# Weight halves kept in DRAM instead of split again: a hybrid S5 / delta-net / ConvFFN step on one core

## The chip, the core and the metric

The kernel runs on one core of a Trainium2 chip. The engines are named as in the profile: PE multiplies matrices (PEld is its weight load), DVE, ACT and POOL work element by element, SP only issues DMAs; 16 DMA engines move data between DRAM and the on-chip memory. The metric is the device time of one launch in microseconds (us). Before the change three runs took 2869.67, 2872.86 and 2876.55 us; their median is 2872.86.

## The reference

One layer of a decoder step on 2048 prompt tokens and 8 sample tokens, all in float32:

```
n = rmsnorm(x);  proj = n @ w_in                       # 1024 -> 2568 columns
y_s5  = s5_mixer(proj[:, :512])                        # state space scan, then gelu and a gate (s5_w_glu)
y_gdn = gdn_mixer(proj[:, 512:])                       # q, k, v, z of 4 heads: delta rule in chunks
x = x + concat(y_s5, y_gdn) @ w_out                    # 1024 x 1024
h = causal_conv(rmsnorm(x) @ w_up)                     # 1024 -> 2 * 2816, width 3
y = rmsnorm(x + (silu(h_gate) * h_up) @ w_down)        # 2816 -> 1024
```

The states of the scan, of the delta rule and of the convolutions are outputs too.

## The kernel before

The prompt is worked in four quarters of 512 tokens; quarter 0 carries the 8 samples behind its tokens and is multiplied in two blocks of 256 and 264 columns, the others in one of 512. Norm 1 and the S5 inputs of all quarters come first, then the S5 batches beside the delta net of quarter 0, then (from about 560 us) the output gate, output projection and FFN of one quarter after the other, with the delta net of the next quarters beside them. The orders of emission are the strings `PRE`, `MIXERS` and `FFN`; a scheduler that simulates the engines makes the order of each queue from them, so the order on an engine is fixed before the kernel runs.

A float32 product is made of three matmuls on two halves of each operand: hi (rounded) and lo (the rest), hi*hi + hi*lo + lo*hi (`mm3`, L287 to L289). Weights come in tiles of 128 x 1024. For each use of a tile `wsplit` loads the raw tile into `wr` (512 KB, issued by SP from L303 for columns of a matrix, from L1082 for rows of w_down), ACT copies it to `whi` (L71), and DVE, or POOL in the early part, subtracts to get `wlo` (L72). There are 2 buffers `wr` and 8 buffers for halves, so 4 tiles split and 2 raw ones ahead. A tile is used for 24 matmuls of 512 columns (48 half as wide in quarter 0). Each quarter loads and splits its tiles anew:

- w_in for q, k, v and z of 4 heads: 16 tiles per quarter (`gdn_front`);
- the gate s5_w_glu: 4 tiles for each two quarters (`s5_glu`);
- w_out: 8 tiles for each half of a quarter's tokens (`ffn_out`), so 16 per quarter;
- w_up: 44 tiles and w_down: 22 tiles per quarter (`ffn`, `ffn_down`). In quarters 1 to 3 four of the w_up tiles are used for the first half of the tokens and once more for the second (`UPS`).

With the 4 tiles of the S5 input that makes 404 splits. The buffers for halves (`c.W`) also hold other things: `gdn_sample` (L984) puts the samples' states (`S0s`, 4 loads for a first product and 4 more for the new states) and `vd` into them, `sample_halos` its raw rows. SP's queue works in order: an issue whose buffer isn't free holds all behind it, the small DMAs of the delta net's inverse (`nD`, `N`, `xD`, `T2T`, `gdn_inverse`) among them.

Of the kernel before, what the change touches and what calls it, by code (L numbers as in the profile page):

```python
# [20 lines left out]
QT = 512            # tokens per quarter  # L21
NQ = QT + 8         # the first quarter carries the 8 samples behind its tokens
NCH = 256           # S5 chunks of 8 tokens
# [14 lines left out]
# order of emission. u: next tile of the S5 input projection, l: samples' halos, c: columns of the first  # L38
# quarter; b, h: first and second part of the next S5 batch, x: S5 samples; F, I, B: front, inverse and back
# of the next delta net head, N: norm and columns of the next quarter, S: delta net samples, G: final states;  # L40
# r: next piece of the output gate, the output projection and the FFN
# [3 lines left out]
# columns of the constants  # L45
# [3 lines left out]
def f32(ap):  # L49
    return ap.bitcast(F32)  # L50
# [18 lines left out]
def split(nc, hi, lo, raw, eng=None):  # L69
    """hi + lo == raw exactly, both float32r."""  # L70
    nc.scalar.activation(hi, raw, AF.Copy)  # L71
    (eng or nc.vector).tensor_tensor(lo, raw, f32(hi), op=OP.subtract)  # L72


def sigmoid_(nc, out, x, scale=1.0):
    """out = sigmoid(scale*x) by exp and ln; 1/(1+inf) = 0 comes out of exp(-ln inf)."""
    nc.scalar.activation(out, x, AF.Exp, scale=-scale)
    nc.scalar.activation(out, out, AF.Ln, bias=1.0)
    nc.scalar.activation(out, out, AF.Exp, scale=-1.0)


def rsqrt_(nc, a, y, t):
    """y = a^-1/2; one Newton step after exp/ln."""
# [9 lines left out]
def rsqrt_cols(c, ss, n, scale, tag, rows=128, tmp=None):  # L93
    """(ss*scale + eps)^-1/2 for ss [rows, n]"""
# [6 lines left out]
# ---------------------------------------------------------------- constants  # L101
def consts(c):
# [13 lines left out]
    # per-channel weights as columns  # L116
# [17 lines left out]
    # GDN  # L134
# [4 lines left out]
    # w_in columns for beta, a: [hi 8 | lo 8] per k tile  # L139
# [15 lines left out]
    # Xi[p, r, i] = (i == 4 (p % 8) + r): four rows of a 32 x 32 identity per partition  # L155
# [8 lines left out]
def sample_halos(c):  # L164
    """contribution of the samples' conv states to their conv outputs: [channel, sample]"""
# [24 lines left out]
# ---------------------------------------------------------------- norm 1  # L190
def norm_split(c, nT, kt, src, g, rsB, b0, b1):
    """nT[kt] <- hi, lo of src * g[channel] * rsB[token]"""
# [13 lines left out]
def norm_first(c, q, nT, xs):  # L206
    """x^T and its row scales to DRAM, x^T times the channels' weights into nT; the row scales are
    in it only in the first quarter, elsewhere they come after the projection"""
# [26 lines left out]
    # row scales on all partitions  # L235
# [13 lines left out]
def norm_samples(c, pre):  # L249
    """normed x^T of the samples, [channel, (k tile, sample)]"""  # L250
# [41 lines left out]
def wsplit(c, src, eng=None):  # L292
    """[128, 1024] of weights as hi and lo"""
    hi, lo, wr = c.W("whi"), c.W("wlo"), c.WR("wr")
    src(wr)
    split(c.nc, hi, lo, wr, eng or c.wl)
    return hi, lo


def wcols(c, w, col, q=None):  # L300
    """w[:, col:col+128] as hi and lo, [128, k, 128]"""
    def load(wr):
        (q or c.nc.sync).dma_start(wr.rearrange("p (k f) -> p k f", k=8), w.rearrange("(k p) f -> p k f", p=128)[:, :, col:col + 128])  # L303
    return [t.rearrange("p (k f) -> p k f", k=8) for t in wsplit(c, load)]
# [7 lines left out]
def proj(c, q, nT, w, col):  # L312
    """w[:, col:col+128]^T n, one PSUM tile per block of tokens"""
# [12 lines left out]
# ---------------------------------------------------------------- S5  # L326
def cmul(nc, pool, outr, outi, ar, ai, br, bi, shape, tag):
    """(outr + i outi) = a*b; outputs must not alias inputs."""
# [16 lines left out]
def s5_setup(c):  # L345
    """S5 matrices to DRAM: per batch of 4 groups T, F (input), E (output), tables."""
# [5 lines left out]
    c.ab1 = cp.tile([128, 2, 32], F32, name="ab1")   # re | signed im (-, +)  # L352
    with tc.tile_pool(name="s5b", bufs=1, side="right") as sp:
# [3 lines left out]
        def dup_T(ap, name):  # L357
            """[32, 64] dram -> [128 (n twice), 32]"""
# [18 lines left out]
        # angle to [-pi, pi]  # L377
# [18 lines left out]
        # powers of a-bar: PR, PI [128, 32, 9]  # L396
# [13 lines left out]
        # f  # L410
# [14 lines left out]
        # W = f B  [128 (n twice), 32, 16]  # L425
# [9 lines left out]
        # C transposed [128 (n twice), 512 (g c)]  # L435
# [13 lines left out]
        # signed power tables  # L449
        PA = sp.tile([128, 32, 9], F32, name="PA")  # L450
        PB = sp.tile([128, 32, 9], F32, name="PB")
        QA = sp.tile([128, 32, 8], F32, name="QA")   # powers 7 .. 0
# [14 lines left out]
        # d on the diagonal: rows 112..127 of K_0  # L467
# [7 lines left out]
        for b in range(8):  # L475
# [4 lines left out]
            def outer(eng, dst, x, xp, y, yp):  # L480
                # dst[p, g, l, c] = x[p, g, c]*xp[p, g, l] + y[p, g, c]*yp[p, g, l]
# [7 lines left out]
            FTs = st("FTs")   # [.., g, s, c'] = a^(7-s) f B  # L489
# [14 lines left out]
            pT = ps("s")    # [(s c'), j, g, c]  # L504
# [6 lines left out]
        # rotation tables  # L511
# [9 lines left out]
        for b in range(4):  # L521
            gs = slice(8 * b, 8 * b + 8)
            CSt = sp.tile([128, 2, 8, 65], F32, name="CSt")     # cos | signed sin (+ | -)
# [14 lines left out]
def s5_in(c, q, nT, pre, ws, rsB):  # L538
    """u to DRAM, time as (position in chunk, chunk)"""
# [19 lines left out]
def s5_states(c, sp):  # L559
    """samples: inputs and states of all groups"""  # L560
# [6 lines left out]
    c.h0 = sp.tile([128, 2, 32, 8], F32, name="h0")      # [re | im , im | re]  # L567
# [13 lines left out]
def s5_gelu(c, sp, out, y, rows=128):  # L581
    """gelu(y) = y sigmoid(2 sqrt(2/pi) (y + 0.044715 y^3))"""
# [13 lines left out]
def s5_turn(c, e, Ct, St, out):  # L596
    """out = the states e of a quarter's end, rotated back"""
# [10 lines left out]
def s5_batch(c, t, sp):  # L608
    """4 groups (64 channels) over all prompt tokens, and their samples"""
# [19 lines left out]
    # chunk inputs, rotated  # L629
# [13 lines left out]
    # scans in place, a quarter at a time  # L643
# [8 lines left out]
    # the rotation back of the last state, and of the states in two parts for the two products with E  # L652
# [5 lines left out]
    # outputs  # L658
# [13 lines left out]
    # samples  # L672
# [13 lines left out]
def s5_sample(c, sp):  # L686
# [5 lines left out]
    # new state = x + a h0  # L692
# [20 lines left out]
def s5_glu(c, q0, yT):  # L713
    """output gate of two quarters"""
# [12 lines left out]
    for a in range(4):  # L727
# [5 lines left out]
        h4, l4 = (v(t) for t in wsplit(c, load))  # L733
# [25 lines left out]
# ---------------------------------------------------------------- gated delta net  # L759
def gdn_cols(c, q, nT):  # L760
    """per-token columns: 0 beta, 1 g, 2 -gc, 3 e^gc, 4 e^(gl-gc), 5 e^gl, 6 -e^gc"""
# [26 lines left out]
    nc.vector.scalar_tensor_tensor(t_, m_, -2.0, xa_, op0=OP.mult, op1=OP.add)   # -|x|  # L788
# [20 lines left out]
def gdn_front(c, q, h, nT, col, hp):  # L809
    """projections, conv, norms, decay: L^T, A^T, scaled k and v of one head"""  # L810
# [31 lines left out]
    # transposes to token-major  # L842
# [11 lines left out]
    # head columns: 0 rk, 1 rq*d^-1/2, 2 nk, 3 -rk^2 beta, 4 rk e^(gl-gc), 5 beta rk, 6 rq'^2/128  # L854
# [14 lines left out]
    # decay  # L869
# [20 lines left out]
def gdn_inverse(c, h, LT, T):  # L890
    """(I - L)^-1 transposed for the 4 chunks of a head: 32-blocks by substitution (four rows of a
    block per partition), then merged to 64 and 128."""
# [18 lines left out]
    # merge 32 -> 64 -> 128  # L911
# [33 lines left out]
def gdn_back(c, q, h, col, F, T):  # L945
    """chunk recurrence, output norm and gate of one head"""
# [20 lines left out]
    # output norm and gate  # L967
# [16 lines left out]
def gdn_sample(c, col):  # L984
    """one step of the delta rule for the 8 samples of all heads; columns are (head, sample)"""
# [6 lines left out]
    # kS, qS  # L992
# [10 lines left out]
    # sums over channels, and per-sample scalars, on every partition  # L1003
# [11 lines left out]
    # v_new = beta (v - e^g rk kS)  # L1015
# [4 lines left out]
    # o = rq' (e^g qS + (q.k) rk v_new)  # L1020
# [5 lines left out]
    # norm and gate  # L1026
# [7 lines left out]
    # states: e^g S + k v_new^T  # L1034
# [30 lines left out]
def sample_conv_out(c, new, nt, old, out):  # L1065
    """conv states of the samples: the old one shifted, and the new row"""
# [13 lines left out]
# ---------------------------------------------------------------- output projection and FFN  # L1080
# [373 lines left out]
```

## Time and profile before

| | |
|---|---|
| median of three runs | 2872.86 us |
| span of the profiled execution | 2874.3 us |
| PE busy | 2715.0 us, 94% |
| DVE busy | 2176.9 us, 76% |
| ACT busy | 1476.0 us, 51% |
| DMA, mean of the span | 115 GB/s |

The profiled execution's span is 1.4 us above the median of the runs and inside their range. PE is busy for nearly the whole of the stretches inside a quarter from about 840 us on; its granted clock there is 1.00 of its full speed. Before that, in the S5 and first delta net part, both are lower. The boundaries between the quarters of the FFN lie near 1300 to 1440, 1900 to 2000 and 2400 to 2480 us.

### The profile page before, as it was taken

Reading aid. Unit: us, or ns where it says so; the run is one execution under the profiler, and the core shown is the slowest. Engines: PE = TensorE matmul, PEld = TensorE weight load, DVE = VectorE, ACT = ScalarE, POOL = GpSimd, SP = SyncE. Lnnn points to the kernel's source line nnn. Section 1 sums busy time; section 2 is a strip of 40 time slices with the busy share of each in tenths; the row PEclk is TensorE's granted clock in tenths of the full one; section 3 lists DMA queues with packets and bytes.
Section 4 is the critical chain, followed back from the end, with each engine's and each line's share of the span. In section 5 each row is a group of like instructions: output and inputs, shape, how many; then the busy total and the mean of one; then the engine's idle time right before and its main releaser. Section 6 shows DMA issues by size and latency. Waiting matters only on the chain.

```text
span 2874.3 us, 45554 instructions
## 1 busy us (share of the span) xinstructions
PE 2715.0 (94%) x16103; PEld 2337.9 (81%) x16103; DVE 2176.9 (76%) x4964; ACT 1476.0 (51%) x3051; POOL 609.6 (21%) x970
## 2 busy tenths in 40 slices
PE   6998788899999999998899999999999998999998
PEld 4798676786888999998887888878888787888887
DVE  8949898856688787778588687887768667676666
ACT  4446565653665554455564554555545445444444
POOL 4325332100121122222221100113211112211112
PEclk9999887898999999999999999999999999999999
DMA  7644433453644232233533333245333334523332
GB/s 205 199 134 132 113 109 92 105 133 104 182 110 117 77 103 87 89 97 111 155 115 109 100 91 98 84 137 174 93 96 97 90 93 144 157 88 96 95 97 74
DMA packets 457657, 329.30 MB, mean 115 GB/s; under 512 B 74960, under 2 KB 412249, under 8 KB 457412
## 3 DMA queue, kind: packets, MB, share of 16 engines
q1 hardware_dynamic: 447091, 297.77, 35.8%
q0 software_dynamic: 10336, 28.61, 3.4%
q8 instruction: 127, 2.08, 0.3%
q14 instruction: 103, 0.84, 0.1%
HBM read 279.29 MB, written 47.29 MB: 114 GB/s over the span
## 4 chain that ended last, share of the span: by engine, by line
PE 66%; DVE 17%; DMA 8%; ACT 4%; issue 3%; POOL 0%; SPq 0%; DVEq 0%; POOLq 0%; ACTq 0%
PE psmm L287 15%; PE psmm L288 15%; PE psmm L289 15%; PE psd L287 5%; PE psd L288 5%; PE psd L289 5%; DVE wlo L72 3%; DVE t L823 1%; ACT whi L71 1%; DVE X L907 1%; DMA xr<-xTD 1%; DMA mr<-mixT 1%; DVE x L1097 1%; DVE hh L649 1%; DMA wr<-in_w_out_dram 1%
## 5 line engine op out<-in xcount | busy, mean ns | idle before, releaser
L287 PE MATMUL psmm<-nT,whi 128*128 128x512 f32 (+2 forms) x3232 | 1115.5, 347 | 45.2 <-ACT whi L71 9.6
L288 PE MATMUL psmm<-nT,whi 128*128 128x512 f32 (+2 forms) x3232 | 1110.3, 344 | 4.8 <-DVE nT L224 3.0
L289 PE MATMUL psmm<-nT,wlo 128*128 128x512 f32 (+2 forms) x3232 | 1107.2, 343 | 1.7 <-POOL wlo L72 1.0
L287 PEld LDWEIGHTS psmm<-nT,whi 128*128 128x128 f32 x3232 | 622.5, 193 | 120.3 <-ACT whi L71 11.7
L288 PEld LDWEIGHTS psmm<-nT,whi 128*128 128x128 f32 x3232 | 624.5, 193 | 73.1 <-DVE nT L224 4.5
L71 ACT ACTIVATE whi<-wr 128x1024 fp32r<-128x1024 f32 x404 | 427.2, 1059 | 496.3 <-PE psmm L288 309.9
L289 PEld LDWEIGHTS psmm<-nT,wlo 128*128 128x128 f32 x3232 | 623.0, 193 | 72.4 <-issue 1.9
L72 DVE TENSOR_TENSOR wlo<-wr,whi 128x1024 fp32r<-128x1024 f32 x388 | 482.3, 1246 | 193.2 <-ACT whi L71 187.4
L1097 DVE TENSOR_TENSOR x<-psd,x 128x512 f32<-128x512 f32 (+2 forms) x464 | 255.6, 558 | 127.3 <-PE psd L289 125.2
L287 PE MATMUL psd<-gt,whi 128*128 128x512 f32 (+2 forms) x928 | 323.6, 350 | 12.7 <-DVE x L1097 10.4
L288 PE MATMUL psd<-gt,whi 128*128 128x512 f32 (+2 forms) x928 | 316.5, 342 | 0.0
L289 PE MATMUL psd<-gt,wlo 128*128 128x512 f32 (+2 forms) x928 | 314.6, 340 | 0.0
L1254 DVE SCALAR_TENSOR_TENSOR t<-raw,cc,t 128x512 f32<-128x512 f32 x352 | 271.5, 772 | 37.1 <-ACT t L1251 27.5
L1255 POOL COPY halo<-raw 128x2 f32<-128x2 f32 x176 | 49.6, 282 | 850.7 <-DVE raw L1250 765.9
L1251 ACT ACTIVATE t<-raw,cc 128x512 f32<-128x512 f32 (+1 forms) x176 | 127.2, 723 | 170.0 <-DVE raw L1250 156.7
L287 PEld LDWEIGHTS psd<-gt,whi 128*128 128x128 f32 x928 | 175.0, 189 | 42.5 <-DVE x L1097 18.8
L72 POOL TENSOR_TENSOR gt<-s,gt 128x512 fp32r<-128x512 f32 (+1 forms) x88 | 134.7, 1531 | 350.4 <-ACT gt L71 341.6
L288 PEld LDWEIGHTS psd<-gt,whi 128*128 128x128 f32 x928 | 175.1, 189 | 20.6
L289 PEld LDWEIGHTS psd<-gt,wlo 128*128 128x128 f32 x928 | 174.9, 189 | 20.8
L1107 POOL TENSOR_TENSOR sq<-sq 128x256 f32<-128x256 f32 (+1 forms) x112 | 109.8, 981 | 219.1 <-ACT sq L1105 213.1
L906 DVE TENSOR_TENSOR tm<-X,N 128x124 f32<-128x124 f32 (+30 forms) x496 | 125.4, 253 | 26.7 <-DMA N<-nD 17.6
L907 DVE TENSOR_TENSOR X<-X,tm 128x124 f32<-128x124 f32 (+30 forms) x496 | 129.6, 261 | 8.4
(503 smaller groups left out, 3666.5 us busy)
## 6 DMA issues: line engine op xcount, KB each, us to landing
wr<-in_ffn_w_up_dram SPq DMA_DIRECT2D x176, 512.0 KB
wr<-in_ffn_w_down_dram SPq DMA_DIRECT2D x88, 512.0 KB
wr<-in_w_in_dram SPq DMA_DIRECT2D x64, 512.0 KB
wr<-in_w_out_dram SPq DMA_DIRECT2D x64, 512.0 KB
xTD<-xT SPq DMA_DIRECT2D x32, 256.0 KB
N<-nD SPq DMA_DIRECT2D x16, 512.0 KB
mr<-mixT SPq DMA_DIRECT2D x32, 256.0 KB
xr<-xTD SPq DMA_DIRECT2D x32, 256.0 KB
```

The lines of the kernel that those rows point to most:

```text
L71: nc.scalar.activation(hi, raw, AF.Copy)
L72: (eng or nc.vector).tensor_tensor(lo, raw, f32(hi), op=OP.subtract)
L287: nc.tensor.matmul(out, lhsT=wh, rhs=xh, start=first, stop=False)
L288: nc.tensor.matmul(out, lhsT=wh, rhs=xl, start=False, stop=False)
L289: nc.tensor.matmul(out, lhsT=wl, rhs=xh, start=False, stop=last)
L906: nc.vector.tensor_tensor(m, X[:, :, j:j + 1].to_broadcast(sh), N[:, j:j + 1, j + 1:].to_broadcast(sh), op=OP.mult)
L907: nc.vector.tensor_tensor(X[:, :, j + 1:], X[:, :, j + 1:], m, op=OP.add)
L1097: nc.vector.tensor_tensor(x2[:, j, b0:b1], p, x2[:, j, b0:b1], op=OP.add)
L1107: c.nc.gpsimd.tensor_tensor(acc[0], acc[0], s, op=OP.add)
L1251: nc.scalar.activation(t[:, :n], raw[:, 2:2 + n], AF.Copy, scale=w[2])
L1254: nc.vector.scalar_tensor_tensor(t[:, :QT], raw[:, j:j + QT], w[j], t[:, :QT], op0=OP.mult, op1=OP.add)
L1255: nc.gpsimd.tensor_copy(c.halo[:, ch], raw[:, QT:QT + 2])
```

## The change

A hi and a lo half now share one buffer of 128 x 2 x 1024, of which there are 4 (`c.W2`). The first time that a tile of w_in (q, k, v, z), s5_w_glu, w_up or w_down is split, SP also stores both halves to a DRAM tile of 1 MB; when a later quarter asks for the same tile, one DMA of 1 MB loads both halves, and there is no raw load and no split. That makes 86 stores and 250 loads of halves. w_out and the S5 input's tiles are not kept: they are loaded raw and split as before. What used one of the 8 buffers (`S0s`, `vd`, the raw rows of `sample_halos`) now takes the first half of one of the 4. Comments are dropped too, so line numbers shift by 8 or so.

```diff
-def wsplit(c, src, eng=None):
-    hi, lo, wr = c.W("whi"), c.W("wlo"), c.WR("wr")
-    src(wr)
-    split(c.nc, hi, lo, wr, eng or c.wl)
-    return hi, lo
+def wsplit(c, src, key=None):
+    nc = c.nc
+    w = c.W2("w2")
+    if key in c.kept:
+        nc.sync.dma_start(f32(w), f32(c.kept[key]))
+    else:
+        wr = c.WR("wr")
+        src(wr)
+        split(nc, w[:, 0], w[:, 1], wr, c.wl)
+        if key is not None:
+            c.kept[key] = c.wdr.tile([128, 2, 1024], F32R, name="k%d" % len(c.kept))
+            nc.sync.dma_start(f32(c.kept[key]), f32(w))
+    return w[:, 0], w[:, 1]
...
-def wcols(c, w, col, q=None):
+def wcols(c, w, col, q=None, keep=True):
...
-    return [t.rearrange("p (k f) -> p k f", k=8) for t in wsplit(c, load)]
+    return [t.rearrange("p (k f) -> p k f", k=8) for t in wsplit(c, load, (w.tensor.name, col) if keep else None)]
...
-        h4, l4 = (v(t) for t in wsplit(c, load))
+        h4, l4 = (v(t) for t in wsplit(c, load, ("glu", a)))
...
-    return wsplit(c, lambda wr: c.nc.sync.dma_start(wr, w[r0:r0 + 128, :]))
+    return wsplit(c, lambda wr: c.nc.sync.dma_start(wr, w[r0:r0 + 128, :]), (w.tensor.name, r0))
...
-        mm24(c, p, wcols(c, c.w_out, j * 128), nT, b0, b1)
+        mm24(c, p, wcols(c, c.w_out, j * 128, keep=False), nT, b0, b1)
...
-        c.W = lambda name, dt=F32R: wp.tile([128, 1024], dt, name=name, tag="w", bufs=NW)
+        c.W2 = lambda name, dt=F32R: wp.tile([128, 2, 1024], dt, name=name, tag="w", bufs=NW // 2)
+        c.W = lambda name, dt: c.W2(name, dt)[:, 0]
+        c.kept = {}
...
-            ws = [wcols(c, c.w_in, t * 128, WQ(nc)) for t in range(4)]
+            ws = [wcols(c, c.w_in, t * 128, WQ(nc), False) for t in range(4)]
```

What it moves on SP in the FFN of quarter 0, once w_up and w_down stream; of before (a row is the line, the operation, out<-in, its shape and how many follow each other):

```order
L1082 DMA wr<-in_ffn_w_down_dram 128x1024 x2
L303 DMA wr<-in_ffn_w_up_dram 128x8x128 x4
L1082 DMA wr<-in_ffn_w_down_dram 128x1024 x2
L303 DMA wr<-in_ffn_w_up_dram 128x8x128 x4
L1082 DMA wr<-in_ffn_w_down_dram 128x1024 x2
```

and now, where `k_...` is a kept DRAM tile and `w_...` a buffer of halves:

```order
L304 DMA k_11585<-w_11580 128x2048
L1090 DMA wr<-in_ffn_w_down_dram 128x1024
L304 DMA k_11653<-w_11648 128x2048
L1090 DMA wr<-in_ffn_w_down_dram 128x1024
L304 DMA k_11728<-w_11723 128x2048
L311 DMA wr<-in_ffn_w_up_dram 128x8x128
L304 DMA k_11735<-w_11730 128x2048
L311 DMA wr<-in_ffn_w_up_dram 128x8x128
```

Ahead of each raw load now stands the store of a tile split before; both wait for the same split.

On SP in the FFN of quarter 3, before:

```order
L303 DMA wr<-in_ffn_w_up_dram 128x8x128 x4
L1082 DMA wr<-in_ffn_w_down_dram 128x1024 x2
L303 DMA wr<-in_ffn_w_up_dram 128x8x128 x4
L1082 DMA wr<-in_ffn_w_down_dram 128x1024 x2
L303 DMA wr<-in_ffn_w_up_dram 128x8x128 x4
```

and now:

```order
L297 DMA w_26028<-k_10221 128x2048
L297 DMA w_26064<-k_10289 128x2048
L297 DMA w_26109<-k_10366 128x2048
L297 DMA w_26145<-k_10434 128x2048
L297 DMA w_26188<-k_10509 128x2048
L297 DMA w_26190<-k_10516 128x2048
```

Each load of six now goes straight into a buffer of halves, and can be issued only when PE is done with the tile that was there.

On POOL, the samples' states in `gdn_sample`, before:

```order
L824 COPY gh<-raw 128x3
L991 DMA S0s<-in_state_gdn_dram 128x8x128 x8
L1033 DMA mixT<-sst 128x4x8
L1051 DMA out_dram<-S0s 128x8x128 x4
L821 COPY raw<-gh 128x3
```

and now:

```order
L999 DMA S0s<-in_state_gdn_dram 128x8x128 x6
L1041 DMA mixT<-sst 128x4x8
L999 DMA S0s<-in_state_gdn_dram 128x8x128
L1059 DMA out_dram<-S0s 128x8x128
L999 DMA S0s<-in_state_gdn_dram 128x8x128
L1059 DMA out_dram<-S0s 128x8x128 x3
```

Two of the eight loads have moved behind later steps: they wait for buffers that the first heads' new states give back.

## Rows read from the trace of the kernel before

**Rows 1.** The page's head: the span, and each engine's busy time, share and instructions.

```profile
span 2874.3 us, 45554 instructions
...
PE 2715.0 (94%) x16103; PEld 2337.9 (81%) x16103; DVE 2176.9 (76%) x4964; ACT 1476.0 (51%) x3051; POOL 609.6 (21%) x970
```

**Rows 2.** By stage: window, length, busy PE, PEld, DVE, ACT, POOL; clock, DMA share, GB/s.

```profile
560.00:840.00 280.00, 264.89 (x1499) 220.86 (x1499) 197.30 (x534) 143.14 (x334) 37.08 (x48) 0.92 0.48 133
840.00:1300.00 460.00, 456.87 (x3596) 435.39 (x3595) 360.93 (x852) 238.58 (x480) 104.67 (x204) 1.00 0.33 93
1300.00:1440.00 140.00, 124.63 (x901) 114.24 (x900) 100.69 (x222) 74.84 (x155) 35.48 (x49) 0.95 0.47 139
1440.00:1900.00 460.00, 455.99 (x2321) 371.11 (x2321) 369.80 (x816) 243.36 (x492) 61.76 (x127) 1.00 0.34 99
1900.00:2000.00 100.00, 92.74 (x646) 84.51 (x645) 75.93 (x150) 56.48 (x110) 29.41 (x37) 0.97 0.56 170
2000.00:2400.00 400.00, 399.45 (x1928) 328.82 (x1927) 292.35 (x493) 199.50 (x352) 58.00 (x119) 1.00 0.34 101
2400.00:2480.00 80.00, 66.56 (x473) 62.69 (x474) 54.42 (x97) 38.76 (x69) 29.87 (x33) 0.91 0.55 167
```

**Rows 3.** The page's costliest groups: the split, with count, busy us, mean ns, idle before.

```profile
L71 ACT ACTIVATE whi<-wr 128x1024 fp32r<-128x1024 f32 x404 | 427.2, 1059 | 496.3 <-PE psmm L288 309.9
...
L72 DVE TENSOR_TENSOR wlo<-wr,whi 128x1024 fp32r<-128x1024 f32 x388 | 482.3, 1246 | 193.2 <-ACT whi L71 187.4
```

**Rows 4.** PE's waits on splits, at 1300-1440, 1900-2020, 2370-2520: us, times, longest.

```profile
PE psmm L287 <- ACT whi L71: 3.1, 1, 3.1
...
PE psmm L287 <- ACT whi L71: 1.4, 2, 1.1
...
PE psmm L287 <- ACT whi L71: 5.2, 2, 3.0
```

**Rows 5.** By window, what touches `wlo`: PE, PEld, DVE (the splits), POOL; clock, DMA.

```profile
1300.00:1440.00 140.00, 70.48 (x233) 45.36 (x232) 30.96 (x24) 0.00 (x0) 0.95 0.47 139
1900.00:2000.00 100.00, 52.78 (x171) 33.18 (x170) 25.22 (x20) 0.00 (x0) 0.97 0.56 170
2400.00:2480.00 80.00, 42.68 (x143) 29.45 (x143) 20.25 (x16) 0.00 (x0) 0.91 0.55 167
```

**Rows 6.** Two windows of 72 us, in the FFN of quarter 0 and of 3.

```profile
1078.00:1150.00 72.00, 72.00 (x627) 70.86 (x626) 50.56 (x91) 31.41 (x50) 18.08 (x36) 1.00 0.30 88
2587.00:2659.00 72.00, 72.00 (x312) 58.22 (x311) 48.11 (x66) 33.38 (x51) 9.66 (x22) 1.00 0.31 95
```

**Rows 7.** The page's DMA issues, weight tiles: line, queue, count, size.

```profile
wr<-in_ffn_w_up_dram SPq DMA_DIRECT2D x176, 512.0 KB
wr<-in_ffn_w_down_dram SPq DMA_DIRECT2D x88, 512.0 KB
```

**Rows 8.** PE's timeline at the samples, the gate tile's matmuls: start us, length us.

```profile
691.14 0.79 PE L287 MATMUL psmm<-nT,whi 128*128 128x512 f32 x1
...
706.97 0.39 PE L289 MATMUL psmm<-nT,wlo 128*128 128x512 f32 x1
```

**Rows 9.** POOL's timeline there, stores of the new states, with the idle time before.

```profile
692.45 0.90 POOL L1051 DMA_DIRECT2D out_dram<-S0s  x1 [1.30 <-DVE S0s L1050]
698.97 0.89 POOL L1051 DMA_DIRECT2D out_dram<-S0s  x1 [5.62 <-DVE rv L957]
...
711.62 0.89 POOL L1051 DMA_DIRECT2D out_dram<-S0s  x1 [2.57 <-DVE S0s L1050]
```

**Rows 10.** Tile `S0s`, eight loads of 512 KB.

```profile
DMA to landing us min/median/max: 3.8/4.8/8.7
```

**Rows 11.** Waits of the whole span: DVE for the inverse's matrix `N`.

```profile
DVE tm L906 <- DMA N<-nD: 17.6, 9, 3.7
```

**Rows 12.** The window of 10 us in which the DMA engines moved most.

```profile
80.00:90.00 10.00, 9.92 (x62) 8.13 (x61) 9.88 (x25) 3.63 (x7) 3.24 (x5) 1.00 0.89 321
```

**Rows 13.** The page's DRAM traffic.

```profile
HBM read 279.29 MB, written 47.29 MB: 114 GB/s over the span
```

More of the change, by code (lines that the diff above doesn't have):

```diff
@@ L1303 @@
         c.cp, dr = pool("c"), pool("dr", space=DRAM)
+        c.wdr = dr
         wp, vp, np_ = pool("w"), pool("v"), pool("n")
```

## The prediction, made before the changed kernel ran

> **What bounds the kernel now.** I read the page's head first. PE is busy for 94% of a span of 2874.3 us, no other engine for more than 76% [rows 1]; so the question for every edit is whether PE waits less or more. The table by stage shows where it waits at all. Inside the quarters' FFNs there is nearly no idle PE: 460 − 456.87 = 3.1 us in 840 to 1300, 4.0 in 1440 to 1900, 0.6 in 2000 to 2400, and the clock is 1.00. Idle PE is in 560 to 840 (15.1 us) and at the three boundaries between quarters: 15.4, 7.3 and 13.4 us, 36 us together, where the clock falls to 0.91 to 0.97 [rows 2]. A reader should see that a split can cost time only in those stretches. Third come the costliest groups: the 404 copies to `whi` keep ACT busy for 427.2 us, and most of ACT's idle time before them, 309.9 us, is a wait for PE to give a buffer back [rows 3]. So ACT isn't late; it is held by PE. Last are PE's own waits at the boundaries: for `whi` 3.1, 1.4 and 5.2 us, 9.7 us in all [rows 4].
>
> **What goes away.** Of 404 splits 250 are replaced: 82 tiles (16 of w_in, 44 of w_up, 22 of w_down) in each of three quarters are 246, and 4 of the gate. ACT loses 250 × 1.059 = 265 us, DVE 250 × 1.246 = 312 us [rows 3], and 250 raw loads of 512 KB go (w_up and w_down: three quarters of 176 and 88 [rows 7], 198 of them). In the interiors this hides under PE and is worth nothing: PE has 0.6 us of idle time in 400 there [rows 2]. At the boundaries 24, 20 and 16 splits stand [rows 5], 60 in all, and 48 of these are w_out's, which the change doesn't keep. So 12 of 60, a fifth of the 9.7 us of waits, go: −2 us. Before 840 only the second call of the gate and some of quarter 1's w_in are replaced, and I take −1 us out of 15.1 us idle. Bounds for the two together: 0, and −20 us (below, as a rival). Sum: −3.
>
> **What is added on the DMAs.** 86 stores of 1.05 MB are 90 MB on 47 MB written; 250 loads grow by 0.52 MB each, 131 MB on 279 read [rows 13]. The loads first, since each now has a new wait. Before, a raw tile was loaded ahead into one of two `wr`, and the split followed when PE gave halves back. Now a load can be issued only when PE is done with the tile that lay in the buffer; behind it on SP wait all later issues, weight tiles and the delta net's small transfers alike. How far ahead is that? In the FFN 312 matmuls of 512 columns take 72 us [rows 6], 231 ns each, so a tile of 24 takes 5.5 us. Counting in PE's order from the last matmul of a tile to the first one of the tile that takes its buffer, the shortest distance in a steady group of six tiles is 36 matmuls, 8.3 us. A load of 1 MB isn't in this trace. The nearest row is `S0s`, 512 KB, with 4.8 us to landing, 3.8 at least and 8.7 at most [rows 10]. The busiest window moved 321 GB/s at a share of 0.89 [rows 12]; at a more usual 290 (133 ÷ 0.48 is 277, 170 ÷ 0.56 is 304 [rows 2]) another 0.52 MB take 1.8 us. That makes 6.6 us, within 5.6 to 10.5. I take 6.6, from the median of the row: it lands 1.7 us before it is wanted, cost 0. The bounds are 0 and 10.5 − 8.3 = 2.2 us for a late tile.
>
> The Trainium skill (DMA: Bandwidth & Descriptors, section "Latency and other measured facts") puts the latency of DRAM at 0.2 us on average and at 2 us under high load. By it a load in a busy stretch would land up to 1.8 us later, at an estimated 8.4 us, and the margin would be gone; the sum would be that of the slower rival. The `S0s` row shows a spread wider than that, 4.9 us between its ends, at 512 KB [rows 10]; it does not tell latency from queueing.
>
> The stores: in the FFN of quarter 0, 48 matmuls of a tile take 48 × 72 ÷ 627 = 5.5 us [rows 6], and in that time 0.52 MB are loaded and 1.05 MB stored, 1.57 MB: at 277 to 304 GB/s 5.2 to 5.7 us, at 321 4.9. The 16 engines are then 89 to 103% busy. A store only holds a buffer, for which PE's 24 matmuls of the earlier tiles give cover, so I take 0; if the DMAs are the slower, 66 tiles × up to 0.5 us = +33 us at the other end.
>
> The delta net's transfers (`N`, `T2T`, `xD`) stand on the same queue and engines; one may now come behind 1 MB in place of 512 KB, 1.8 us later. DVE waited for `N` 9 times, 17.6 us [rows 11]; 9 × 1.8 = 16 us is the upper bound, 0 the lower, and as PE is fed beside it in most of these places I take +2.
>
> **What the pairing moves.** Four pairs in place of eight single buffers hold as many tiles, but `S0s` and `vd` now take a whole pair each. So in `gdn_sample` loads 7 and 8 wait for pairs that earlier heads give back, as POOL's order shows. The first store of new states is issued at 692.45, the last at 711.62 [rows 9]. A load behind the first store lands at about 692.5 + 0.9 + 4 (the store) + 5 [rows 9, 10], some 702, early enough for the last head; but the gate's tile, whose matmuls now lie between 691.14 and 706.97 among the samples' own [rows 8], gets its buffer only after a store has landed, at about 707, and all 8 of the samples' matmuls come ahead of it on PE. What filled PE's gaps there then stands behind them: 24 matmuls × 231 ns [rows 6] = 5.5 us, I take +5; bounds 0 (the chain of the new states hides it) and +12 (24 at the 0.5 us that the slow clock gives here: 0.79 and 0.39 are the two rows of [rows 8]).
>
> **Sum.** −3 + 0 (loads) + 0 (stores) + 2 + 5 = +4 us. The profiled span is 2874.3 us, 1.4 above the median of the runs; on the median, 2872.86 + 4 = 2877. This case's own range is 2867 to 2885.
>
> **Rivals.**
> - *The loads land late (slower).* The mechanism: issue only after PE's release, 8.3 us of distance, and a landing that is over that in part of the cases. It decides where a landing of 1 MB takes more than 8.3 us. In three quarters there are 3 × 11 groups of six tiles. If one load in three is late by the 2.2 us worked out above, or each by a third of it, this is 33 × 0.73 = +24 us: 2901. For it speaks the 8.7 us at 512 KB, and that SP holds all else behind a waiting load; against it the share of 0.31 of the DMA engines in the interior [rows 6], which leaves them free when the load comes.
> - *The stores make the DMAs the bound in quarter 0 (slower).* At 0.1 to 0.5 us for each of 66 tiles, +7 to +33; the middle is 2877 + 18 = 2895. For it: 89 to 103% by the sum above. Against it: DVE and ACT are held by PE there, so that stores have slack of some tiles.
> - *The freed engines shorten the boundaries (faster).* ACT was blocked in front of splits for 309.9 us and DVE for 187.4 [rows 3], in order, so that the delta net's and norms' steps stood behind a split that waited for PE. With those gone, PE's idle 36 us at the boundaries and 15 before 840 [rows 2] could shrink by a third to a half, −20: 2853. Against it: w_out's splits stay, and they are 48 of the 60 there.
>
> **How the numbers follow.** Chances: the forecast 0.34, late loads 0.26, stores 0.12, freed engines 0.26, something else 0.02. A measurement of this kernel tells 0.2% apart, 5.7 us, so "within" is 2867.2 to 2878.6. Of the forecast's 0.34 I put 0.28 inside and 0.05 above, 0.01 below; of the others 0.03 fall within (a small gain, few late loads). Faster 0.26, within 0.31, slower 0.43. The range of 8 in 10: below, 2850 takes in most of the faster case; above, 2918 takes in 2901 and 2895 with both mechanisms in part (2877 + 24 + 18 = 2919). So 2850 to 2918.
>
> **What the profile after would show.** Copies to `whi` 154, subtractions on DVE 138; DRAM writes near 137 MB, reads near 410. If the forecast holds: PE idle in 1440 to 1900 and 2000 to 2400 still under 5 us, waits "PE ← DMA w" few and short, landing of the 1 MB loads under 8 us, the stretch at 690 to 715 some 5 us longer. Late loads would show as waits of PE for DMA into `w`, 0.5 to 2 us each, spread over quarters 1 to 3. A DMA bound would show as a DMA share over 0.95 in 860 to 1300 and PE idle there. The faster rival would show the boundaries at 15, 7 and 13 us idle shrunk, the chain there no longer through `whi` and `wlo`. I am wrong if PE's busy time itself changes, or if the delta net's chain, not PE, sets a quarter's end.

## The result and the profile after

The changed kernel takes 2901.11 us (median of 4 runs, 2899.72 to 2901.46) against 2871.70 for the kernel before on the same chip: a ratio of 1.0093, interval [1.0079, 1.0108], slower. That is inside the range of 2850 to 2918, but 24 us above the forecast of 2877, and it is, to the microsecond, the time of a rival whose mechanism the trace does not show. That the range holds it is luck: its upper end was set by late loads and by stores that saturate the DMA engines, and neither came.

The page of the changed kernel, in the order of the page: span, busy time, DMA share in 40 slices, DRAM traffic, the two halves of the split, and the DMA issues.

```profile
span 2897.9 us, 44817 instructions
...
PE 2720.8 (94%) x16103; PEld 2336.4 (81%) x16103; DVE 1907.4 (66%) x4714; ACT 1246.3 (43%) x2801; POOL 556.8 (19%) x970
...
DMA  7648743553667577777565554555555445545553
...
HBM read 410.36 MB, written 137.47 MB: 189 GB/s over the span
...
L71 ACT ACTIVATE w<-wr 128x1024 fp32r<-128x1024 f32 x154 | 162.6, 1059 | 160.9 <-PE psmm L289 80.0
...
L72 DVE TENSOR_TENSOR w<-wr,w 128x1024 fp32r<-128x1024 f32 x138 | 170.9, 1239 | 76.5 <-ACT w L71 76.1
...
w<-k SPq DMA_DIRECT2D x250, 1024.0 KB
k<-w SPq DMA_DIRECT2D x86, 1024.0 KB
```

The work went as the diff says: 154 copies in place of 404, 138 subtractions in place of 388 [rows 3], ACT 230 us and DVE 270 us less busy than before [rows 1], DRAM traffic up by 131 and 90 MB [rows 13]. PE's work is the same, 16103 matmuls; they take 2720.8 us in place of 2715.0. Yet the span is 23.6 us longer, so 17.8 of these are idle PE. Where? One table by stage can't say, since the windows shift; an instruction that both kernels have can. Such a one is DVE's addition of w_down's products to `x`, 464 of them, from the first of the FFN of quarter 0 to nearly the end of the kernel. First the kernel before, then the changed one (count; minimum, median and longest duration in ns; first and last start in us).

```profile
L1097 DVE TENSOR_TENSOR x<-psd,x x464: 405/678/694, 888.4 to 2862.1; 128x512 f32<-128x512 f32 x81, 128x256 f32<-128x256 f32 x44, 128x264 f32<-128x264 f32 x30
```

```profile
L1105 DVE TENSOR_TENSOR x<-psd,x x464: 406/678/694, 908.0 to 2885.4; 128x512 f32<-128x512 f32 x81, 128x256 f32<-128x256 f32 x44, 128x264 f32<-128x264 f32 x30
```

The first is 19.6 us late, the last 23.3. So by this mark 84% of the loss is there before the first FFN result, in the S5, delta net and samples' part, before any weight tile of the FFN has been read back; the four quarters of the FFN together lose 3.7 us. A single mark moves by some us with the order around it; a second one, the output projection's addition (L1144 before, L1152 now), is 17.0 us late at its first start and 20.3 at its last:

```profile
L1144 DVE TENSOR_TENSOR x<-psmm,xr x64: 405/423/433, 749.1 to 2490.4; 128x256 f32<-128x256 f32 x56, 128x264 f32<-128x264 f32 x8
```

```profile
L1152 DVE TENSOR_TENSOR x<-psmm,xr x64: 408/425/433, 766.1 to 2510.7; 128x256 f32<-128x256 f32 x56, 128x264 f32<-128x264 f32 x8
```

That the early part is written in another order can be seen in it. The last result of an S5 batch (`yv`) now starts 23.7 us earlier, and the factor that the delta net's first output is scaled by (`ro_y`) 20.5 us later; before, then now:

```profile
L593 DVE TENSOR_TENSOR yv<-pss,ga x16: 639/678/692, 271.7 to 514.8; 128x512 f32<-128x512 f32 x16
L974 DVE TENSOR_TENSOR ro_y<-ro_y,hc x16: 146/158/678, 390.2 to 2391.1; 128x4 f32<-128x4 f32 x16
```

```profile
L601 DVE TENSOR_TENSOR yv<-pss,ga x16: 666/684/693, 261.0 to 491.1; 128x512 f32<-128x512 f32 x16
L982 DVE TENSOR_TENSOR ro_y<-ro_y,hc x16: 151/157/165, 410.7 to 2391.5; 128x4 f32<-128x4 f32 x16
```

The table by stage agrees for the interiors (window, length, busy PE, PEld, DVE, ACT, POOL; clock, DMA share, GB/s). The first row is of the kernel before, the others are of the changed one.

```profile
200.00:560.00 360.00, 302.17 (x1924) 261.89 (x1923) 306.91 (x888) 211.86 (x576) 116.83 (x139) 0.86 0.42 114
...
200.00:560.00 360.00, 301.29 (x1885) 259.73 (x1886) 301.92 (x874) 205.44 (x565) 124.25 (x140) 0.85 0.59 176
560.00:840.00 280.00, 256.54 (x1467) 213.26 (x1466) 177.98 (x516) 120.77 (x291) 28.16 (x42) 0.90 0.55 166
840.00:1300.00 460.00, 455.32 (x3524) 429.76 (x3524) 338.26 (x797) 231.53 (x489) 83.85 (x197) 1.00 0.73 236
...
1440.00:1900.00 460.00, 456.95 (x2342) 373.83 (x2341) 294.03 (x743) 184.76 (x436) 48.40 (x125) 0.99 0.53 182
```

PE is idle for 4.7 us in 840 to 1300 (3.1 before) and 3.1 in 1440 to 1900 (4.0) [rows 2], with the DMA engines at 0.73 and 0.53 in place of 0.33 and 0.34. Before 840 it is idle for 23.5 us in 560 to 840 where it was 15.1, and in 200 to 560 for 57.8 before and 58.7 now: that part did not keep PE busy before either. PE's waits in the changed kernel, over the whole span (us, times, longest), name the output projection's addition (L1152) most, splits (`w`, L71) further down, and hardly ever a load of halves:

```profile
PE psmm L287 <- DVE x L1152: 21.2, 13, 6.8
...
PE psmm L287 <- ACT w L71: 11.2, 3, 6.8
...
PE psmm L287 <- DMA w<-k: 1.0, 2, 0.6
```

The first of these grew by 12.7 us, the second by 1.6; in the kernel before they were:

```profile
PE psmm L287 <- ACT whi L71: 9.6, 5, 3.1
...
PE psmm L287 <- DVE x L1144: 8.5, 7, 3.2
```

At the samples, POOL's queue (start, length, idle time before) and PE's:

```profile
702.49 0.89 POOL L999 DMA_DIRECT2D S0s<-in_state_gdn_dram  x1 [1.18 <-PE psf L1056]
703.65 0.89 POOL L1059 DMA_DIRECT2D out_dram<-S0s  x1 [0.26 <-DVE S0s L1058]
708.73 0.88 POOL L999 DMA_DIRECT2D S0s<-in_state_gdn_dram  x1 [4.18 <-DMA out_dram<-S0s]
...
721.48 0.89 POOL L1059 DMA_DIRECT2D out_dram<-S0s  x1 [3.13 <-DVE S0s L1058]
```

```profile
716.28 3.75 PE L1056 MATMUL psf<-vd,skv 32*128 32x512 f32 x4 [2.33 <-DVE vd L1053]
720.83 0.77 PE L287 MATMUL psmm<-nT,w 128*128 128x512 f32 x1
```

The last load does wait 4.18 us for a store to land, and the gate tile now starts behind all of the samples' products, as the prediction had it: at 720.83, where it was done at 706.97 [rows 8]. From the first store of a state to the last it takes 17.8 us, where it took 19.2 [rows 9]; all of it stands 10 us later. What the displaced gate tile costs shows behind it: from the last new state on DVE to the first addition of the output projection (749.1 and 766.1 above) it takes 38.1 us before and 45.3 now.

```profile
L1050 DVE SCALAR_TENSOR_TENSOR S0s<-S0s,sst,psf x32: 328/340/348, 690.0 to 711.0; 128x128 f32<-128x128 f32 x32
```

```profile
L1058 DVE SCALAR_TENSOR_TENSOR S0s<-S0s,sst,psf x32: 329/342/349, 700.5 to 720.8; 128x128 f32<-128x128 f32 x32
```

### The profile page after: what moved, and what is told of

It is laid out like the page before. It is cut to its first block, busy times and chain, and to the rows that moved or that the text cites. A ratio compares the mean times of both kernels' runs of the same rounds, so it can differ in the third digit from the quotient of the medians.

```text
span 2897.9 us, 44817 instructions
## 1 busy us (share of the span) xinstructions
PE 2720.8 (94%) x16103; PEld 2336.4 (81%) x16103; DVE 1907.4 (66%) x4714; ACT 1246.3 (43%) x2801; POOL 556.8 (19%) x970
## 4 chain that ended last, share of the span: by engine, by line
PE 70%; DVE 14%; DMA 8%; ACT 3%; issue 2%; POOL 1%; SPq 1%; ACTq 0%; DVEq 0%; POOLq 0%
PE psmm L287 16%; PE psmm L288 16%; PE psmm L289 16%; PE psd L287 5%; PE psd L288 5%; PE psd L289 5%; DMA wr<-in_w_out_dram 2%; DVE w L72 2%; DMA xr<-xTD 2%; DVE X L915 1%; DVE x L1105 1%; DVE hh L657 1%; DVE tm L914 1%; ACT w L71 1%; DMA mr<-mixT 1%
## 5 line engine op out<-in xcount | busy, mean ns | idle before, releaser
L287 PE MATMUL psmm<-nT,w 128*128 128x512 f32 (+2 forms) x3232 | 1114.7, 347 | 55.9 <-DVE x L1152 21.2
L288 PE MATMUL psmm<-nT,w 128*128 128x512 f32 (+2 forms) x3232 | 1108.0, 343 | 4.8 <-DVE nT L224 3.0
L289 PE MATMUL psmm<-nT,w 128*128 128x512 f32 (+2 forms) x3232 | 1103.9, 342 | 1.4 <-POOL w L72 1.2
L287 PEld LDWEIGHTS psmm<-nT,w 128*128 128x128 f32 x3232 | 620.2, 192 | 131.7 <-ACT w L71 18.4
L288 PEld LDWEIGHTS psmm<-nT,w 128*128 128x128 f32 x3232 | 622.9, 193 | 72.7 <-DVE nT L224 4.5
L289 PEld LDWEIGHTS psmm<-nT,w 128*128 128x128 f32 x3232 | 620.7, 192 | 71.0 <-POOL w L72 1.5
L287 PE MATMUL psd<-gt,w 128*128 128x512 f32 (+2 forms) x928 | 324.4, 350 | 16.0 <-DVE x L1105 15.1
L1262 DVE SCALAR_TENSOR_TENSOR t<-raw,cc,t 128x512 f32<-128x512 f32 x352 | 270.0, 767 | 87.2 <-ACT t L1259 81.9
L288 PE MATMUL psd<-gt,w 128*128 128x512 f32 (+2 forms) x928 | 316.6, 341 | 0.0
L289 PE MATMUL psd<-gt,w 128*128 128x512 f32 (+2 forms) x928 | 314.6, 340 | 0.0
L1257 ACT ACTIVATE raw<-psmm 128x256 f32<-128x256 f32 x170 | 65.5, 385 | 452.5 <-PE psmm L289 450.9
L71 ACT ACTIVATE w<-wr 128x1024 fp32r<-128x1024 f32 x154 | 162.6, 1059 | 160.9 <-PE psmm L289 80.0
L1258 DVE TENSOR_TENSOR raw<-psmm,rs 128x256 f32<-128x256 f32 (+1 forms) x170 | 72.4, 426 | 234.7 <-ACT raw L1257 208.5
L72 DVE TENSOR_TENSOR w<-wr,w 128x1024 fp32r<-128x1024 f32 x138 | 170.9, 1239 | 76.5 <-ACT w L71 76.1
L287 PEld LDWEIGHTS psd<-gt,w 128*128 128x128 f32 x928 | 174.7, 188 | 47.1 <-DVE x L1105 23.9
L72 POOL TENSOR_TENSOR gt<-s,gt 128x512 fp32r<-128x512 f32 (+1 forms) x88 | 118.2, 1344 | 403.9 <-ACT gt L71 403.8
L288 PEld LDWEIGHTS psd<-gt,w 128*128 128x128 f32 x928 | 175.0, 189 | 20.7
L289 PEld LDWEIGHTS psd<-gt,w 128*128 128x128 f32 x928 | 174.5, 188 | 21.3
L831 DVE SCALAR_TENSOR_TENSOR t<-raw,cc,t 128x512 f32<-128x512 f32 x144 | 119.0, 827 | 48.8 <-ACT t L828 45.7
```

Of the source, the lines that this page charges most:

```text
L287: nc.tensor.matmul(out, lhsT=wh, rhs=xh, start=first, stop=False)
L288: nc.tensor.matmul(out, lhsT=wh, rhs=xl, start=False, stop=False)
L289: nc.tensor.matmul(out, lhsT=wl, rhs=xh, start=False, stop=last)
L831: nc.vector.scalar_tensor_tensor(t[:, :QT], raw[:, j:j + QT], w[j], t[:, :QT], op0=OP.mult, op1=OP.add)
L1257: nc.scalar.activation(raw[:, 2:2 + b0], ps[0][:, :b0], AF.Copy)
L1258: nc.vector.tensor_tensor(raw[:, 2 + b0:2 + b1], ps[-1][:, -(b1 - b0):], rsB, op=OP.mult)
```

## The experiments

Each was run five rounds beside the kernel before. What the table shows for all: median, ratio to the kernel before with its interval, and by how much the first and the last of those 464 additions start later than in the kernel before (888.4 and 2862.1 us).

| kernel | median us | ratio | first | last |
|---|---|---|---|---|
| changed kernel | 2901.1 | 1.0093 [1.0079, 1.0108] | +19.6 | +23.3 |
| 1 pairs only | 2895.7 | 1.0066 [1.0049, 1.0083] | +13.0 | +19.4 |
| 2 w_in not kept | 2895.3 | 1.0065 [1.0048, 1.0082] | +13.9 | +21.6 |
| 3 stores only | 2908.5 | 1.0119 [1.0101, 1.0136] | +26.1 | +28.0 |
| 4 stores from POOL | 2935.5 | 1.0205 [1.0186, 1.0224] | +34.5 | +44.4 |
| 5 pairs only, packed | 2898.7 | 1.0074 [1.0059, 1.0090] | +20.1 | +23.4 |
| 6 changed, packed | 2908.7 | 1.0104 [1.0086, 1.0121] | +19.8 | +21.3 |
| 7 kept, single buffers | 2894.9 | 1.0082 [1.0062, 1.0102] | +15.9 | +16.8 |
| 8 as 7, w_in not kept | 2886.8 | 1.0034 [1.0022, 1.0046] | +6.6 | +12.3 |
| 9 before, products reordered | 2898.9 | 1.0087 [1.0074, 1.0100] | +12.7 | +26.7 |
| 10 before, three fills | 2882.7 | 1.0031 [1.0020, 1.0043] | +0.5 | -3.1 |
| 11 as 5, products reordered | 2890.8 | 1.0068 [1.0048, 1.0088] | +8.0 | +13.2 |
| 12 as 5, three fills | 2904.3 | 1.0101 [1.0086, 1.0115] | +21.0 | +28.2 |

The medians of the kernel before in these sets were 2875.38 (1 to 4), 2875.07 (5 to 8) and 2872.96 (9 to 12). The sets ran on different chips, so kernels of different sets are compared by their ratios. The offsets are those of the one profiled execution, which in 3, 4, 6 and 10 is the fastest of its runs, 4 to 11 us below the median.

**1. Pairs only.** Nothing is stored or read back; 404 splits, as before.

```diff
-        if key is not None:
+        if False:
```

> Halves in pairs as in the changed kernel, but nothing is kept: no stores, no loads of halves, 404 splits as before. Theory A (the trace of the changed kernel is 14 us behind at 555 us and 18 behind at 840, and only 4 to 5 more from there on: the 16 stores of w_in tiles, 1 MB each between 205 and 330 us, delay the S5 and delta net part, and the samples' stage adds some 6): 2878 us, with the 6 us of the samples' stage left. Theory B (the pairing alone moves the order and holds buffers longer): 2895 to 2901. Theory C (loads of halves land late in quarters 1 to 3): 2872.

2895.7 us: theory C (late loads) is out, since no load is left, and A has 17 us unexplained. B's 2895 to 2901 holds. Two thirds of the loss come with the pairs alone.

```profile
L1105 DVE TENSOR_TENSOR x<-psd,x x464: 381/679/694, 901.4 to 2881.5; 128x512 f32<-128x512 f32 x81, 128x256 f32<-128x256 f32 x44, 128x264 f32<-128x264 f32 x30
```

**2. w_in not kept.**

```diff
-    return projw(c, q, nT, wcols(c, w, col))
+    return projw(c, q, nT, wcols(c, w, col, keep=w is not c.w_in))
```

> The changed kernel, but w_in's 16 tiles are not kept: they are loaded raw and split in every quarter; w_up, w_down and the gate are kept. Theory A: the stores between 205 and 330 us are gone, so about 2901 - 14 = 2887 us, and the lag at 555 us is near 0. Theory B: 2901. Theory C: 202 of 250 loads of halves stay, so about 2896.

2895.3: between A's 2887 and B's 2901. It is C's 2896, but the first experiment has ruled C out. Leaving out w_in's 16 stores and 48 loads gives back about 0.3%, and most of the loss stays.

**3. Stores only.** Every quarter splits again; the stores stay.

```diff
-    if key in c.kept:
+    if False:
...
-        if key is not None:
+        if key is not None and key not in c.kept:
```

> The changed kernel with its 86 stores, but later quarters load raw and split again: no loads of halves. Theory A: 2901 us, within 4. Theory B: 2901. Theory C: 2872 to 2876, since no load of halves is left. If splits in the later quarters did cost time, it is above 2901.

2908.5, above A's 2901 within 4. It lies 13 us over the first experiment, and 13 of these are there at the first FFN result (+26.1 against +13.0). In 200 to 560 us no engine's waits for one kind of transfer add up to more than 2.8 us, so that the stores' traffic does it isn't shown; the last set gives another cause. Nor do the splits that are back in the later quarters explain a time above 2901: from the first FFN result to the last this kernel loses 1.9 us, the changed one 3.7.

**4. Stores from POOL's queue.**

```diff
-            nc.sync.dma_start(f32(c.kept[key]), f32(w))
+            nc.gpsimd.dma_start(f32(c.kept[key]), f32(w))
```

> The changed kernel with the 86 stores issued from POOL's queue in place of SP's, so that no store stands on SP ahead of raw loads and of the small transfers. If in theory A it is SP's order that costs (a store waits for POOL's or DVE's lo half, and all behind it with it): about 2888 us, lag at 555 us under 5. If it is the traffic (DMA share 0.80 to 0.85 in 200 to 280 us against 0.59 and 0.48 before): 2901, lag as it is. Theory B: 2901.

2935.5, worse than either case. The stores stand on an engine that works: POOL waits for DVE's half, and behind the waiting store stand its own norms and halos. Its rows (issues: ns min, median, max; then waits of POOL: us, times, longest):

```profile
L304 POOL DMA_DIRECT2D k<-w x86: 532/564/622, 204.3 to 1364.3; - x86
```

```profile
POOL k L304 <- DVE w L72: 78.8, 22, 8.9
```

So POOL's queue costs more than SP's, which does nothing but issue DMAs. What the stores cost on SP isn't shown by this, since the move brought a cost of its own; that the pairs' 20 us are not theirs is shown by the first experiment, which has no store.

**5 and 6. Packed pairs.** The samples' states, `vd` and the halos' rows take half a pair each, in the kernel of the first experiment and in the changed one.

```diff
-        S0 = mat("S0s").rearrange("p (b e) -> p b e", b=8)
+        sw = c.W2("S0s", F32)
+        S0 = sw[:, 0].rearrange("p (b e) -> p b e", b=8)
...
-        vd = mat("vd")[:32].rearrange("p (b e) -> p b e", b=8)
+        vd = sw[:32, 1].rearrange("p (b e) -> p b e", b=8)
```

> As the first experiment (pairs, nothing kept), but the samples' states, vd and the raw rows of the halos are packed two to a pair, so that they take as much of the four pairs as they took of the eight single buffers. Theory B1 (what else uses the buffers now takes twice as much; that is the 20 us of the first experiment): 2875 to 2879 us. Theory B2 (a pair comes free and is handed out as one, which moves the written order everywhere): 2890 to 2898, no change.

> The changed kernel with the same packing. Theory B1: 2901 - 20 = 2881 us, the samples' stage at 690 to 715 us back to its length of before. Theory B2: 2897 to 2903.

2898.7 and 2908.7: theory B1 is wrong, and B2's bounds are passed by 1 and 6 us. The doubled use of the buffers at the samples isn't what the 20 us are. It does have a price: packed, the gate tile's matmuls lie among the samples' own again, and from the last new state to the output projection's first addition run 6 takes 40.7 us, where the changed kernel took 45.3.

```profile
L1065 DVE SCALAR_TENSOR_TENSOR S0s<-S0s,sst,psf x32: 328/341/348, 702.4 to 723.8; 128x128 f32<-128x128 f32 x32
...
L1159 DVE TENSOR_TENSOR x<-psmm,xr x64: 405/424/433, 764.5 to 2509.4; 128x256 f32<-128x256 f32 x56, 128x264 f32<-128x264 f32 x8
```

The same stretch takes 41.7 to 45.3 us in the five kernels with pairs that are not packed (the changed one, 1 to 4) and 35.7 to 40.7 in all others. The total shows no gain from it, as the packed kernels come to the samples later.

**7 and 8. The halves kept, eight single buffers.** In 8 w_in isn't kept.

```diff
-    w = c.W2("w2")
+    w = [c.W("whi"), c.W("wlo")]
...
+        for i in range(2):
+            nc.sync.dma_start(f32(w[i]), f32(c.kept[key][:, i]))
```

> The halves are kept in DRAM as in the changed kernel, but in the eight single buffers of before: a store and a load are two DMAs of 512 KB each. If pairing is most of the loss (theory B, either kind): 2875 + 7 = 2882 us, the 7 being what the changed kernel lies above the first experiment. If DMAs are (theory A or C), 2895 to 2905; twice as many issues on SP's queue could add to it.

> As the run before it, but w_in isn't kept, so that no store falls into the S5 and delta net part. Additive with the second experiment (6 us below the changed kernel): 2876 us, no slower than the kernel before. If stores and loads of w_up and w_down cost time by themselves: 2882 or more.

2894.9 and 2886.8. Without pairs the loss should have been 7 us and is 20, the time that was put down for DMAs; and 8 is the mildest form of the change, 0.34%. The losses of pairing and keeping do not add. Not keeping w_in helps here too (0.48%): the first FFN result is 6.6 us late in 8, 15.9 in 7. By what was expected of 8, a time above 2882 stands for stores and loads of w_up and w_down that cost by themselves. Its loss does arise behind the samples, 1.8 us ahead at the output projection's first addition and 10.7 late at the last (749.1 to 2490.4 before), but the next set shows losses of that size in the same place without any store, so it isn't told apart.

```profile
L1154 DVE TENSOR_TENSOR x<-psmm,xr x64: 406/424/433, 747.3 to 2501.1; 128x256 f32<-128x256 f32 x56, 128x264 f32<-128x264 f32 x8
```

**9 to 12. The written order.** Up to here each version had lost 7 to 35 us at the first FFN result, by whatever it differed. What they share is that the scheduler wrote their queues anew. SP's queue around the first inverse, in the kernel before and in the first experiment (the same DMAs; shifted line numbers):

```
L303 DMA wr<-in_w_in_dram 128x8x128 x7
L897 DMA nD_83<-LT 32x4x32 x4
L303 DMA wr<-in_w_in_dram 128x8x128
L899 DMA N<-nD_83 128x1x1024
L303 DMA wr<-in_w_in_dram 128x8x128
```

```
L311 DMA wr<-in_w_in_dram 128x8x128
L905 DMA nD_83<-LT 32x4x32 x4
L628 DMA tab<-tabD 128x520
L629 DMA Tm<-TD 128x512
L630 DMA Em<-ED 128x512
L907 DMA N<-nD_83 128x1x1024
L311 DMA wr<-in_w_in_dram 128x8x128 x2
```

`N` now stands behind three tables of the S5 batch. The tables alone cost little: from the first `nD` to the first `N` it takes 4.4 us (273.0 to 277.4) in place of 2.9 (257.0 to 259.9), while `nD` itself is 16 us late. Aligned as lists by their longest common stretches, 47% of DVE's 4964 instructions keep their place in the first experiment, 71% in run 9 and 95% in run 10. Run 9 exchanges two matmuls of every product, run 10 adds three fills that nothing reads; 11 and 12 do the same to run 5.

```diff
-    nc.tensor.matmul(out, lhsT=wh, rhs=xl, start=False, stop=False)
-    nc.tensor.matmul(out, lhsT=wl, rhs=xh, start=False, stop=last)
+    nc.tensor.matmul(out, lhsT=wl, rhs=xh, start=False, stop=False)
+    nc.tensor.matmul(out, lhsT=wh, rhs=xl, start=False, stop=last)
```

```diff
             c.wl = W1(nc)
+            for _ in range(3):
+                jt = c.V("jt")
+                nc.vector.memset(jt, 0.0)
```

> The kernel before, with nothing of the change: only the last two of the three matmuls of a product are written in the other order (hi*hi, lo*hi, hi*lo), the same work and the same eight buffers. The scheduler then writes another order of the engines' queues from the first projections on. Theory O (the loss of the pairs is the other written order, not a buffer held longer: the order of before is a good one among many, another one with the same work costs 5 to 30 us): 2880 to 2900 us. Theory P (a pair that is handed out and given back as one costs the time): 2875 us within 4.

> The kernel before with three extra fills of a scratch tile on DVE (about 1 us) ahead of the projections, which nothing reads; 97% of PE's instructions keep their written order. Theory O: between 2875 and 2885 us, less than the run before it since the order moves less. Theory P: 2876.

> The fifth experiment (pairs, other users packed, nothing kept; 2898.7 us) with the order of the last two matmuls of a product exchanged as in the first run of this set. Theory O: another draw, anywhere from 2880 to 2910, with no reason to be at 2899. Theory P: 2899 within 4.

> The fifth experiment (2898.7 us) with three extra fills of a scratch tile on DVE ahead of the projections. Theory O: another draw, 2880 to 2910. Theory P: 2899 within 4.

Run 9 has nothing of the change and is as slow as the changed kernel: 1.0087. Its rows and those of the fills:

```profile
L1097 DVE TENSOR_TENSOR x<-psd,x x464: 406/678/693, 901.1 to 2888.8; 128x512 f32<-128x512 f32 x81, 128x256 f32<-128x256 f32 x44, 128x264 f32<-128x264 f32 x30
```

```profile
L1367 DVE MEMSET jt<- x3: 498/498/498, 4.0 to 5.1; 128x528 f32 x3
```

Three fills of 498 ns, 1.5 us at the start, cost 9.7 us at the median; its runs spread from 2872.99 to 2885.21, and the profiled execution, with a span of 2871.2, stands at the low end, so its offsets are near nothing. The same two edits on the pairs give 2890.8 and 2904.3, by the ratios 2 us below and 8 above run 5, where theory P had 2899 within 4 for both: 12 is outside of that, 11 is not. This is weaker, as the intervals of 11 and 12 just meet and that of 5 overlaps both. Theory O's bounds hold all four. Run 9 is not quite neutral: the lo half is wanted one matmul earlier, 231 ns [rows 6], and it isn't known what part of its 26 us that is. Nor does it lose its time in one part. It is 12.7 us late at the first FFN result and 26.7 at the last; some of the rest goes in quarter 1, where PE is idle for 12.2 us that was idle for 4.0 [rows 2], and the wait for the output projection's addition is 26.5 us, above the 21.2 of the changed kernel:

```profile
1440.00:1900.00 460.00, 447.78 (x2270) 366.56 (x2269) 361.62 (x798) 247.17 (x512) 57.76 (x120) 0.99 0.34 97
```

```profile
PE psmm L287 <- DVE x L1144: 26.5, 10, 6.1
```

## Why the prediction was right and wrong

- **PE bounds the kernel, and splits inside a quarter cost nothing: right.** The freed 230 us of ACT and 270 of DVE gave nothing there; the offset moves from +19.6 to +23.3 over 1977 us. PE's busy time, whose change was a sign of being wrong, rose by 5.8 us, 0.2%. The −3 us for splits that go isn't seen: PE's waits for `whi` in L287's products are 9.6 us in the whole span before and 11.2 now, as w_out's splits stay.
- **Loads of halves land in time: right.** PE waited twice for one, 1.0 us in all. The rival with late loads, 2901, had the time and not the cause: its waits were to spread over quarters 1 to 3, and the loss is there before them. Pairs without any load lose 20 us. No landing of a 1 MB load is in the trace; that they came in time is read from PE's waits.
- **The higher latency under load** that the Trainium skill gives (DMA: Bandwidth & Descriptors, section "Latency and other measured facts"): no run here shows it. In quarter 1, at 182 GB/s (1440 to 1900), and behind it the loads came within the distance that they had, or PE would have waited more than twice.
- **Stores at 0 in the FFN of quarter 0: right there.** DMA share 0.73 where the sum allowed 0.89 to 1.03, PE idle 4.7 us against 3.1. (The rival's middle was a slip: of +7 to +33 it is +20, not +18, which moves the upper end of the range by 2 us.) Ahead of the FFN they were not counted at all, and that was an omission: w_in's 16 tiles are stored from 210 us on. Not keeping w_in gave 0.28% (run 2 against the changed kernel) and 0.48% (run 8 against 7), part or all of which can be order.
- **The delta net's small transfers, +2: wrong sign, small.** DVE waited for `N` 17.6 us before [rows 11], 13.9 now (row below).
- **The samples' stage, +5: right, but looked for in the wrong stretch.** The store-to-load wait and the late gate tile are in the trace. The stretch at 690 to 715 isn't longer; the one behind it is, by 7.2 us, and packing (6) takes 4.6 of these back. It is at most a third of the loss.
- **The freed engines shorten the boundaries: wrong.** PE is idle 18.3, 8.7 and 12.3 us around the three boundaries, 39 us, where in the same windows it was 16.5, 7.3 and 13.6, 37 us (rows below).
- **The step that failed** is the sentence "Four pairs in place of eight single buffers hold as many tiles, but `S0s` and `vd` now take a whole pair each", with all that the sum has for pairing: it priced one place, +5, which came out, and took the rest of the kernel's order as it was, at 0. The pairing alone costs 20 us (2895.7 against 2875.4), 13 of them at the first FFN result. The changed kernel is 9.8 us late at the last new state of the samples (720.8 against 711.0), before the displaced gate tile, the one place that was priced, is multiplied. Ahead of the FFN, where PE was idle for 57.8 of 360 us, and at the output projections PE waits for other engines; that a new written order changes the length of these waits is what run 9 suggests, and it is not shown for the pairs.

The waits of DVE for `N` in the changed kernel, and the boundaries (columns as in the table by stage), three rows of before and three of now:

```profile
DVE tm L914 <- DMA N<-nD: 13.9, 7, 3.0
```

```profile
1300.00:1460.00 160.00, 143.52 (x1050) 132.15 (x1049) 117.32 (x262) 89.55 (x195) 40.41 (x54) 0.96 0.46 137
1900.00:2020.00 120.00, 112.74 (x814) 104.46 (x813) 94.81 (x194) 69.79 (x147) 35.85 (x42) 0.97 0.55 166
2400.00:2520.00 120.00, 106.39 (x768) 100.33 (x769) 85.18 (x145) 61.54 (x111) 39.59 (x47) 0.94 0.50 149
...
1300.00:1460.00 160.00, 141.72 (x1039) 130.49 (x1039) 112.60 (x272) 73.40 (x150) 39.00 (x62) 0.96 0.61 200
1900.00:2020.00 120.00, 111.31 (x726) 97.55 (x725) 79.47 (x159) 57.14 (x113) 31.43 (x43) 1.00 0.55 176
2400.00:2520.00 120.00, 107.71 (x723) 98.05 (x722) 80.32 (x143) 55.02 (x102) 36.73 (x44) 0.96 0.58 194
```

What is shown: the loss isn't late loads, isn't the DMAs' share in the FFN, and the samples' doubled buffers are some 5 to 7 us of it; in the changed kernel it arises mostly ahead of 890 us; two thirds of it come with the pairs, without a store or a load of halves; and edits with nothing of the change in them cost 0.3 and 0.9%. What is argued and not shown: that the pairs' 20 us are, beside the samples' share, the new order and nothing else. For that the pairs would have to run in the written order of before, or that kernel's emission strings be fitted to the pairs again; neither was tried. Until then a part may be the pair that comes free as one; none of the four versions of pairs without keeping is below 0.66%. What the keeping costs by itself, on SP's queue too, stays inside this scatter: four versions of pairs without it lie at 2890.8 to 2904.3, four that store from SP (the changed kernel, 2, 3 and 6) at 2895.3 to 2908.7. No version was faster than the kernel before.

## What to carry to other kernels

Where PE is busy to within 1% of a stretch, taking work off other engines there is worth nothing, and this can be read from one table by stage. Where a scheduler writes the queues, a change of buffers is a change of order in the chain-bound part, however little it touches there: run a neutral edit or two of the old kernel first, and take their scatter (here 10 to 26 us of 2873) as the smallest effect that such a comparison can explain. To find where a loss arises, follow instructions that both kernels have, their first and last start, one or more per stage; here a single one would not have shown the samples' share.

## What was not expected of the hardware

- DMA traffic had little effect on a saturated PE: at 236 GB/s and a share of 0.73 PE was busy 455.3 of 460 us, against 456.9 at 93 GB/s [rows 2].
- A queue on a working engine is dear: the 86 issues take POOL 0.56 us each, 48 us, and it waited 78.8 us in front of them; the same stores cost 1.1%, some 32 us, more there than from SP. Which of the two it is, the issuing or the waiting, isn't told apart.
